# A decoder trunk whose input arrives transposed from the host, with the row norm applied after the first projection

## Chip, core and metric

One core of a Trainium2 chip runs the whole layer in one launch. The metric is device time in microseconds: before, the median of three runs is 781.14 (777.98 to 785.86).

## The reference, cut to what matters

```
u    = x * rsqrt(mean(x*x, -1) + eps) * attn_norm        # x: 1024 rows of 1024
proj = u @ w_in[0]                                       # split into
       # dq dk dv | sq ckv | iq ik iw | rq rk rv | gate
A    = differential attention(dq, dk, dv)                # causal, 6 heads
B    = sparse attention: indexer scores from iq, ik, iw; the 256 best keys of each row
C    = retention(rotary(rq), rotary(rk), rv)             # rotary angles, decays
y    = silu(gate) * concat(A, B, C)
out  = rms_norm(x + y @ w_out[0]) * final_norm
```

Each of the 1024 rows of x has one norm factor. It is common to a whole row, so it can be applied to x before the projection or to a row of the projection after it.

## The kernel before

All products of the projection are made of three matmuls: each operand is split into a high part (rounded to the matmul's format) and a low part (the rest), and high x high, high x low and low x high are added in PSUM. `uh` and `ul` hold the two parts of the normed x, transposed: partitions are 128 of the 1024 model columns (a chunk, k = 0 to 7), free elements are the 1024 rows of x. They stay in SBUF for all units of the projection.

The front. `setup` loads eight row blocks of x (128 rows each, 512 KB) on SyncE's queue; after the second, `wide` puts the weights of the first projection there (columns dv, ik and iw, 456 wide). For each row block `prep_a` squares the rows on ScalarE with a row sum, makes the reciprocal root in `rstd_small` (VectorE and ScalarE in turns on 128x1 operands) and scales the block with norm and gains in one VectorE operation (L213). `prep_b` transposes it with eight TensorE matmuls against the identity into a PSUM tile (L220); ScalarE copies the high part, VectorE subtracts it for the low part (`split`, L113 and L123).

The first projection is unit "a" of `gemm` (L282 to L284): for each row block 24 matmuls with a stationary 128x128 piece of `uh` or `ul` and 456 moving weight columns, accumulated over eight chunks in one PSUM bank. `dv_evac` takes a finished block out: dv and ik by ScalarE (L571, L572), iw by VectorE (L573). After every four blocks the ik part is transposed on TensorE (L578) and split into the keys `kkh` and `kkl`, whose second half of the partitions is filled by two SyncE transfers.

Behind it follow the index units iq0 to iq3 (unit "b" of `gemm`, L130 to L132: 48 matmuls of 512 columns, rows of x as moving operand, in two halves of 512). Their weights come through SyncE and are split on GpSimd (L119, L123). Their results go to DRAM and come back stacked (L305, L318). The index scores (L343, L344) need the keys and iq0. They are interleaved with iq1's successors; then come a top-k search of 31 steps on VectorE and ScalarE, the attention groups with the other units of the projection between them, retention and the output projection.

The order of instructions on each engine is made by a planner that simulates the program with its own costs and picks what is ready by priority. Inside a `manual_schedule` block the named engines keep the order in which the code is written: before, that is TensorE from iq0 to the scores. Tiles of one tag share a number of slots (`bufs`); a new tile waits until the oldest one has been read by all its users. An engine takes its instructions in order, and SyncE and ScalarE each feed a queue of transfers.

Late loads (`setup_late`): small norm vectors, lambda, and a table of rotary angles and decays (`trigdec`, tag `m1`), issued on SyncE.

Of the kernel before, what the change touches and what calls it, by code (L numbers as in the profile page):

```python
# [20 lines left out]
NB = 8  # L21
# [47 lines left out]
class Trunk:  # L69
# [65 lines left out]
    def setup(self):  # L135
        nc, i = self.nc, self.i
        nc.scalar.preload_act_table_set("natural_log_exp_and_others")
        self.ident = self.const("ident", [128, 128])
        make_identity(nc, self.ident)
        self.gb = self.ptile(1024)  # L140
        nc.scalar.dma_start(self.gb, bass.AP(tensor=i["attn_norm"].tensor, offset=i["attn_norm"].offset,
                                             ap=[[0, 128], [1, 1024]]))
        self.x = {}
# [12 lines left out]
        nc.vector.memset(self.ct, 1.0)  # L156
        self.bd = self.const("bd", [128, 128])
        nc.vector.memset(self.bd, 0.0)
        for a in range(2):
            nc.vector.memset(self.bd[a * 64:(a + 1) * 64, a * 64:(a + 1) * 64], 1.0)  # L160

    def setup_late(self):
        nc, i = self.nc, self.i

        def ld(out, in_):
            self.tc.keep_in_program_order(nc.sync.dma_start(out, in_))

# [20 lines left out]
        m1 = self.sb.tile([128, NB, 72], F, name="trigdec", tag="m1")  # L188
        self.trig, self.dec = m1[:, :, 0:64], m1[:, :, 64:72]
        ld(self.trig, i["trig"].rearrange("(b p) c -> p b c", p=128))  # L190
        ld(self.dec, i["decay"].rearrange("(b p) c -> p b c", p=128))

    def rstd_small(self, ss, n, tag):
        nc = self.nc
        w = ss.shape[1]
        t = self.sb.tile([128, 3, w], F, name=self.name("rs"), tag=tag, bufs=2)
        v, r, q = (t[:, j] for j in range(3))
        nc.vector.tensor_scalar(v, ss, 1.0 / n, EPS, op0=OP.mult, op1=OP.add)
        nc.scalar.activation(r, v, AF.Ln)
        nc.scalar.activation(r, r, AF.Exp, scale=-0.5)  # L200
        nc.vector.scalar_tensor_tensor(q, r, v, r, op0=OP.mult, op1=OP.mult)
# [4 lines left out]
    def prep_a(self, b):  # L206
        nc = self.nc
        xt = self.x[b]
        junk = self.half("junk", [128, 1024], BF)
        ss = self.sb.tile([128, 1], F, name=self.name("ss"), tag="ss", bufs=2)  # L210
        nc.scalar.activation(junk, xt, AF.Square, accum_out=ss)
        r = self.rstd_small(ss, D, "rs1")
        nc.vector.scalar_tensor_tensor(xt, xt, r, self.gb, op0=OP.mult, op1=OP.mult)  # L213

    def prep_b(self, b):
        nc = self.nc
        xt = self.x.pop(b)
        p = self.pS()
        for k in range(KC):
            nc.tensor.transpose(p[:, k * 128:(k + 1) * 128], xt[:, k * 128:(k + 1) * 128], self.ident)  # L220
        pv = p.rearrange("p (k s) -> p k s", k=KC)
        sl = slice(b * 128, (b + 1) * 128)
        self.split(self.uh[:, :, sl], self.ul[:, :, sl], pv)

    def wtile(self, base, shape, dt=FR):
        return self.sb.tile([128] + shape, dt, name=self.name(base), tag="w", bufs=NW)
# [2 lines left out]
        return self.sb.tile([128] + shape, F, name=self.name("wr"), tag="wr", bufs=2)  # L229

    def wide(self):
        raws = []
        for k0 in range(0, KC, 2):
            tag, bufs = ("pq", NPQ) if k0 < 2 * NPQ else ("hl", NHL)
            raw = self.sb.tile([128, 2, WA], F, name=self.name("wr"), tag=tag, bufs=bufs)
            for a, b, c in ((0, 384, C_DV), (384, WA, C_IK)):
                self.nc.sync.dma_start(raw[:, :, a:b], self.i["w_in"][
                    0, k0 * 128:(k0 + 2) * 128, c:c + b - a].rearrange("(k p) c -> p k c", p=128))
            raws.append(raw)
        self.dvw = raws  # L240

    def wsplit(self, c0, w):
        hs, ls = [], []
        if w == WA:
# [5 lines left out]
            for k in range(KC):  # L250
                self.split(hs[k], ls[k], self.dvw[k // 2][:, k % 2], *K["s0"][k])
            return hs, ls
        n = 1024 // w
        for k0 in range(0, KC, n):
# [308 lines left out]
    def dv_evac(self):  # L563
        nc = self.nc
        self.v = self.sb.tile([128, NB, 384], F, name=self.name("v"), tag="v")
        self.iw = self.const("iw", [128, NB, 8])
        self.kkh, self.kkl = self.slot("kkh", [128, S], FR), self.slot("kkl", [128, S], FR)
        kt = self.half("kt", [128, NB, 64])

        def evac(b, ps):  # L570
            nc.scalar.activation(self.v[:, b, :], ps[:, 0:384], AF.Copy)  # L571
            nc.scalar.activation(kt[:, b], ps[:, 384:448], AF.Copy)  # L572
            nc.vector.tensor_scalar(self.iw[:, b], ps[:, 448:456], IDX_SCALE, None, op0=OP.mult)  # L573
            if b % 4 == 3:
                sl = slice(b * 128 - 384, b * 128 + 128)
                p = self.pB()
                for j in range(4):
                    nc.tensor.transpose(p[0:64, j * 128:(j + 1) * 128], kt[:, b - 3 + j], self.ident)  # L578
                self.split(self.kkh[0:64, sl], self.kkl[0:64, sl], p[0:64])
            if b == NB - 1:  # L580
                self.mv(self.kkh[64:128], self.kkh[0:64])
                self.mv(self.kkl[64:128], self.kkl[0:64])
        return evac

    def attend(self, pair, stages, GB=2, groups=(3, 2, 1, 0)):
        nc = self.nc
# [244 lines left out]
    def run(self):  # L831
# [148 lines left out]
```

## Time and profile before

| what | value |
|---|---|
| median of three runs | 781.14 us (777.98, 781.14, 785.86) |
| profiled execution | 785.29 us, of which the span of the core is 783.6 |
| TensorE matmul busy | 724.2 us (92%), 4314 instructions |
| VectorE, ScalarE, GpSimd busy | 551.5, 447.6 and 311.5 us |
| moved by DMA | 113.05 MB, mean 144 GB/s |
| granted TensorE clock, mean | 0.974 |

All stretches and dates below are microseconds from the start of the span. In the rows PE is TensorE's matmul, PEld its weight load, DVE is VectorE, ACT is ScalarE, POOL is GpSimd, SPq is SyncE's queue. A matmul's shown duration includes its way through the array, so the pace of a row of matmuls is read from their starts. PEclk is the granted clock as a share of 2.4 GHz.

### The profile page before, as it was taken

The page shows a single profiled execution, that of the slowest core. Times are in us where ns is not written, and L with a number is a line of the kernel's source. Part 1 is how long each engine was busy: PE and PEld are TensorE (multiplying, and loading weights), DVE is VectorE, ACT ScalarE, POOL GpSimd, SP SyncE. Part 2 cuts the span into 40 slices and gives each one's busy share as a digit, 9 for nine tenths or more (in the row PEclk, how much of TensorE's full clock was granted, in tenths as well). Part 3 has the DMA queues.
Part 4 walks back from the last instruction along what each step waited for, and adds up shares of the span by engine and source line. Part 5 has one row for each costly group of instructions (what it writes and reads, how often), then busy time and mean ns, then how long its engine had stood idle before and what let it go on. Part 6 is the DMA issues. An engine that isn't in the chain of part 4 may idle for free.

```text
span 783.6 us, 12891 instructions
## 1 busy us (share of the span) xinstructions
PE 724.2 (92%) x4314; PEld 597.4 (76%) x4314; DVE 551.5 (70%) x1312; ACT 447.6 (57%) x989; POOL 311.5 (40%) x343
## 2 busy tenths in 40 slices
PE   3999999999999999988799789998978999999996
PEld 3798888887887898766577567997855887787884
DVE  5920277789999989999889997325657766664443
ACT  4531255559888968787755566434356656554332
POOL 6401322225434438557347699335733242120000
PEclk9999999999999999999899999999968999999999
DMA  9303645454374352461274476564578974413351
GB/s 332 78 1 71 197 136 145 139 137 132 99 218 115 85 163 78 120 169 35 67 206 144 144 215 190 158 192 160 158 213 236 281 200 127 123 48 108 118 176 59
DMA packets 93250, 113.05 MB, mean 144 GB/s; under 512 B 11904, under 2 KB 63488, under 8 KB 93056
## 3 DMA queue, kind: packets, MB, share of 16 engines
q1 hardware_dynamic: 91888, 109.61, 48.1%
q10 hardware_dynamic: 1296, 2.62, 0.9%
q8 instruction: 34, 0.56, 0.3%
q14 instruction: 32, 0.26, 0.1%
HBM read 75.50 MB, written 36.18 MB: 143 GB/s over the span
## 4 chain that ended last, share of the span: by engine, by line
PE 61%; DVE 16%; DMA 6%; issue 6%; POOL 5%; ACT 4%; SPq 0%; DVEq 0%; POOLq 0%; ACTq 0%
PE pB L626 6%; PE pG L130 6%; PE pG L132 6%; PE pG L131 5%; PE pB L611 4%; PE pG L282 4%; PE pG L936 4%; PE pG L937 4%; PE pG L935 4%; PE pG L283 4%; PE pG L284 4%; DVE jv L378 3%; DMA wr<-in_w_in_dram 2%; PE pS L344 2%; PE pS L343 2%
## 5 line engine op out<-in xcount | busy, mean ns | idle before, releaser
L130 PE MATMUL pG<-uh,wh 128*128 128x512 f32 x352 | 141.6, 402 | 1.8 <-DVE gt L827 1.8
L132 PE MATMUL pG<-uh,wl 128*128 128x512 f32 x352 | 140.7, 400 | 0.6 <-POOL wl L123 0.6
L131 PE MATMUL pG<-ul,wh 128*128 128x512 f32 x352 | 139.4, 396 | 0.0
L123 POOL TENSOR_TENSOR wl<-wr,wh 128x512 fp32r<-128x512 f32 x56 | 79.3, 1430 | 106.3 <-PE pG L131 69.4
L392 ACT ACTIVATE ja<-sc,tk_c 128x896 int8<-128x896 f32 (+2 forms) x93 | 83.2, 895 | 17.3 <-DVE tk_c L399 12.0
L113 ACT ACTIVATE pt<-pB 128x512 f32<-128x512 f32 (+2 forms) x120 | 58.8, 496 | 43.8 <-PE pB L611 43.5
L130 PEld LDWEIGHTS pG<-uh,wh 128*128 128x128 f32 x352 | 66.8, 190 | 16.4 <-DVE gt L827 2.4
L132 PEld LDWEIGHTS pG<-uh,wl 128*128 128x128 f32 x352 | 66.4, 189 | 16.1 <-POOL wl L123 0.9
L611 PE MATMUL pB<-ident,pp 128*128 128x128 f32 x432 | 72.9, 287 | 5.5 <-DVE gt L758 3.4
L626 PE MATMUL pB<-pt,v 128*64 128x128 f32 x864 | 70.8, 302 | 7.6 <-ACT pt L113 7.0
L131 PEld LDWEIGHTS pG<-ul,wh 128*128 128x128 f32 x352 | 66.7, 189 | 13.0 <-issue 0.2
L626 PEld LDWEIGHTS pB<-pt,v 128*64 128x64 f32 x864 | 57.7, 147 | 18.9 <-ACT pt L113 9.5
L378 DVE TENSOR_SCALAR_CACHE_REDUCE jv<-sc,tk_c 128x640 bf16<-128x640 f32 (+4 forms) x81 | 69.2, 855 | 1.0
L611 PEld LDWEIGHTS pB<-ident,pp 128*128 128x128 f32 x432 | 51.2, 144 | 22.2 <-issue 9.1
L677 POOL TENSOR_SCALAR pq<-pq,mx 128x896 f32<-128x896 f32 (+7 forms) x48 | 43.2, 901 | 58.6 <-DVE mx L676 55.8
L119 POOL TENSOR_SCALAR wh<-wr 128x512 fp32r<-128x512 f32 x56 | 37.8, 680 | 59.9 <-DMA wr<-in_w_in_dram 54.3
L282 PE MATMUL pG<-wh,uh 128*128 128x256 f32 x192 | 55.0, 288 | 2.6 <-POOL wh L119 2.6
L283 PE MATMUL pG<-wl,uh 128*128 128x256 f32 x192 | 54.9, 286 | 0.0
L284 PE MATMUL pG<-wh,ul 128*128 128x256 f32 x192 | 54.3, 284 | 0.0
L346 ACT ACTIVATE pp<-pS 128x1024 f32<-128x1024 f32 (+5 forms) x48 | 36.5, 760 | 31.1 <-PE pS L344 31.0
L651 PE MATMUL pS<-st,st 128*128 128x512 f32 (+3 forms) x144 | 43.3, 368 | 11.5 <-DVE mx L662 8.9
L351 DVE SCALAR_TENSOR_TENSOR sc<-pp,iw,sc 128x1024 f32<-128x1024 f32 (+5 forms) x42 | 43.5, 1044 | 14.3 <-ACT pp L346 13.6
(218 smaller groups left out, 1756.1 us busy)
## 6 DMA issues: line engine op xcount, KB each, us to landing
wr<-in_w_in_dram SPq DMA_DIRECT2D x56, 256.0 KB, 3.2
st<-qdq SPq DMA_DIRECT2D x24, 256.0 KB, 4.2
st<-qkk SPq DMA_DIRECT2D x18, 256.0 KB, 5.9
x<-in_x_dram SPq DMA_DIRECT2D x8, 512.0 KB, 6.6
qiq<-hl SPq DMA_DIRECT2D x16, 256.0 KB, 3.5
st<-qiq SPq DMA_DIRECT2D x8, 512.0 KB, 3.3
wr<-in_w_out_dram SPq DMA_DIRECT2D x16, 256.0 KB, 3.4
xr<-in_x_dram SPq DMA_DIRECT2D x8, 512.0 KB, 3.5
```

The source lines that it names most:

```text
L113: self.nc.scalar.activation(out, in_, AF.Copy)
L123: (self.nc.vector if e2 == "v" else self.nc.gpsimd).tensor_tensor(lo, src, hi.bitcast(F), OP.subtract)
L130: mm(ps, wh, xh, start=start, stop=False)
L131: mm(ps, wh, xl, start=False, stop=False)
L132: mm(ps, wl, xh, start=False, stop=stop)
L282: mm(ps, uh, hs[k], start=k == 0, stop=False)
L283: mm(ps, uh, ls[k], start=False, stop=False)
L284: mm(ps, ul, hs[k], start=False, stop=k == KC - 1)
L378: nc.vector.tensor_scalar(jv[:, :nv[b]], hb if b == 7 and bit >= 16 else sc[b], t, 0.0, op0=op, op1=OP.add, accum_out=cnt[:, j:j + 1])
L392: nc.scalar.activation(ja[:, :nv[b]], sc[b], AF.Sign, bias=cut(b), scale=-1.0, accum_out=cnt[:, cols[b]:cols[b] + 1])
L611: nc.tensor.transpose(p[:, k], pr[:, (k0 + k) * 128:(k0 + k + 1) * 128], self.ident)
L626: self.last = nc.tensor.matmul(o[u * 64:(u + 1) * 64], vals[k], pts[g, a][:, k, u * 128:(u + 1) * 128], start=k == (i if u else 0), stop=k ...
```

## The change

- The host passes x transposed as well (`x_t`), `attn_norm` laid out by chunk, and the 456 weight columns of the first projection as one contiguous array (`w_dv`). The latter are loaded on ScalarE's queue, the first two chunks one by one.
- SyncE loads chunk 0 and 1 of `x_t` in halves; then a row block of x behind each further chunk, up to eight. The rows serve the norm alone: ScalarE squares and sums them (`square`).
- `split_x` makes `uh` and `ul` of a chunk from x times gains, without the norm. `front` goes chunk by chunk: six row blocks (18 matmuls a step) accumulate in six PSUM banks at once; then come blocks 6 and 7.
- `diags` makes all norm factors at once, behind the split of the last chunk, and eight diagonal matrices with them; `row_rms` broadcasts the factors over the partitions with eight matmuls.
- `resplit` then scales x by gains and factors and rewrites `uh` and `ul`, half of the columns after blocks 0 to 5, the other half after blocks 6 and 7; iq0 and all later units use these.
- The evictions apply the norm factor and are on ScalarE alone; iw is taken from the ik tile later. The keys' transposes stand behind iq0 (`keys`). Their tile moves to tag `m1`, one slot shared with the table of angles and decays.
- TensorE, VectorE and SyncE keep the written order inside `front`. The weight splits of the first projection use GpSimd and ScalarE, no longer VectorE.

```diff
-K = {... 's0': ('gg', 'gg', 'ag', 'gg', 'vg', 'gg', 'vg', 'vg'), ...
+K = {... 's0': ('gg', 'ag', 'gg', 'ag', 'gg', 'ag', 'gg', 'ag'), ...
...
-        for b in range(NB):
-            self.x[b] = self.slot("x", [128, 1024])
-            nc.sync.dma_start(self.x[b], i["x"][0, b * 128:(b + 1) * 128, :])
-            if b == K["xp"] - 1:
-                self.wide()
+        nc.scalar.dma_start(self.gk, i["attn_norm"])
+        self.wide()
+        self.x, self.rows = [], []
+        self.ss = self.const("ss", [128, NB])
+        for k in range(KC + 1):
+            if k < KC:
+                t = self.slot("x", [128, S])
+                for c in (slice(0, 512), slice(512, S)) if k < 2 else (slice(0, S),):
+                    nc.sync.dma_start(t[:, c], i["x_t"][k * 128:(k + 1) * 128, c])
+                self.x.append(t)
+            for b in ((k - 1,) if 0 < k else ()):
+                row = self.ptile(D) if b % 2 else self.wtile("row", [D], F)
+                nc.sync.dma_start(row, i["x"][0, b * 128:(b + 1) * 128, :])
+                self.rows.append(row)
+                self.square(b)
...
+    def split_x(self, k):
+        g = self.gk[:, k:k + 1]
+        for c in (slice(0, 512), slice(512, S)):
+            hi, x = self.uh[:, k, c], self.x[k][:, c]
+            nc.scalar.activation(hi, x, AF.Copy, scale=g)
+            nc.vector.scalar_tensor_tensor(self.ul[:, k, c], x, g, hi.bitcast(F), op0=OP.mult, op1=OP.subtract)
...
+    def row_rms(self):
+        p = self.pS()
+        for b in range(NB):
+            nc.tensor.matmul(p[:, b * 128:(b + 1) * 128], self.ct, self.dg[b], start=True, stop=True)
+        return p
...
+    def diags(self):
+        self.rn = self.rstd_small(self.ss, D, "rs8")
+        for b in range(NB):
...
+            self.nc.vector.tensor_scalar(self.dg[b], self.ident, self.rn[:, b:b + 1], None, op0=OP.mult)
...
+    def resplit(self, p, half):
+        c = slice(half * 512, half * 512 + 512)
+        for k in range(KC + 1):
+            if k < KC:
+                x = self.x[k][:, c]
+                nc.vector.scalar_tensor_tensor(x, x, self.gk[:, k:k + 1], p[:, c], op0=OP.mult, op1=OP.mult)
+                nc.scalar.activation(self.uh[:, k, c], x, AF.Copy)
+            if k:
+                hi = self.uh[:, k - 1, c]
+                nc.vector.tensor_tensor(self.ul[:, k - 1, c], self.x[k - 1][:, c], hi.bitcast(F), OP.subtract)
...
+    def front(self):
+        big = [self.pS(), self.pS()]
+        ps = [big[b // 2][:, b % 2 * 512:b % 2 * 512 + WA] for b in range(4)] + [self.pB()[:, :WA] for _ in range(2)]
...
+        for k in range(KC):
+            self.split_w(k)
+            self.split_x(k)
+            if k == KC - 1:
+                self.diags()
+            step(range(6), k)
+        for b in range(6):
+            evac(b, ps[b])
+        rb = self.row_rms()
+        self.resplit(rb, 0)
+        ps[6:] = [self.pG()[:, :WA] for _ in range(2)]
+        for k in range(KC):
+            step((6, 7), k)
+        for b in (6, 7):
+            evac(b, ps[b])
+        self.resplit(rb, 1)
...
-            nc.vector.tensor_scalar(self.iw[:, b], ps[:, 448:456], IDX_SCALE, None, op0=OP.mult)
+            nc.scalar.activation(self.v[:, b, :], ps[:, 0:384], AF.Copy, scale=r)
+            nc.scalar.activation(kt[:, b], ps[:, 384:456], AF.Copy, scale=r)
...
-        for b in range(NB):
-            self.prep_a(b)
-            self.prep_b(b)
-        drain(self.gemm(("a", C_DV, WA, self.dv_evac())))
-        with self.tc.manual_schedule(engines={mybir.EngineType.PE}):
-            drain(units("iq0 iq1"))
+        with self.tc.manual_schedule(engines={et.PE, et.DVE, et.SP}):
+            keys = self.front()
+        with self.tc.manual_schedule(engines={et.PE}):
+            drain(units("iq0"))
+            keys()
+            drain(units("iq1"))
```

## Rows read from the trace of the kernel before

**Rows 1.** Page, part 4: shares of the chain that ended last, by engine.
```profile
PE 61%; DVE 16%; DMA 6%; issue 6%; POOL 5%; ACT 4%; SPq 0%; DVEq 0%; POOLq 0%; ACTq 0%
```

**Rows 2.** Windows of the front: stretch, length, busy per engine (count), PEclk, DMA share, GB/s.
```profile
0.00:5.00 5.00, 0.00 (x0) 0.00 (x0) 0.63 (x10) 1.28 (x1) 1.83 (x8) 1.00 0.53 179
5.00:20.00 15.00, 7.84 (x30) 6.98 (x31) 10.58 (x16) 7.64 (x15) 10.61 (x11) 1.00 1.05 384
31.50:36.00 4.50, 4.47 (x19) 3.89 (x20) 4.50 (x17) 2.84 (x7) 0.00 (x0) 0.62 0.02 5
36.00:67.10 31.10, 31.10 (x166) 28.07 (x166) 8.31 (x16) 6.71 (x14) 1.25 (x2) 1.00 0.00 1
```

**Rows 3.** Windows of the score stage and of a later, attention stage.
```profile
100.00:120.00 20.00, 20.00 (x95) 16.72 (x94) 14.28 (x15) 11.18 (x16) 4.81 (x4) 1.00 0.50 151
320.00:360.00 40.00, 33.55 (x185) 25.25 (x182) 37.90 (x98) 33.58 (x79) 18.41 (x21) 0.96 0.44 119
```

**Rows 4.** Timeline of TensorE: start, length, engine, line, operation, tiles.
```profile
15.72 0.73 PE L282 MATMUL pG<-wb,uh 128*128 128x456 f32 x1
...
19.13 0.58 PE L282 MATMUL pG<-wb,uh 128*128 128x456 f32 x2
...
50.22 0.37 PE L283 MATMUL pG<-wb,uh 128*128 128x456 f32 x1
...
56.42 0.37 PE L283 MATMUL pG<-wb,uh 128*128 128x456 f32 x1
...
67.10 0.39 PE L130 MATMUL pG<-uh,wh 128*128 128x512 f32 x1
...
78.36 0.40 PE L130 MATMUL pG<-uh,wh 128*128 128x512 f32 x1
```

**Rows 5.** Timeline of one block's norm and transposes; waits (total, times, longest).
```profile
7.19 0.15 DVE L198 TENSOR_SCALAR rs<-ss 128x1 f32<-128x1 f32 x1 [5.53 <-ACT junk L211]
...
8.49 1.28 DVE L213 SCALAR_TENSOR_TENSOR x<-x,rs,pp 128x1024 f32<-128x1024 f32 x1
...
24.03 1.07 PE L220 MATMUL pS<-ident,x 128*128 128x128 f32 x8
...
PE pS L220 <- DVE rs L198: 11.0, 2, 9.9
```

**Rows 6.** Timeline: first data, late loads, iq1's weights; median landing of weight loads.
```profile
6.01 1.06 ACT L211 ACTIVATE junk<-x 128x1024 bf16<-128x1024 f32 x1 [3.93 <-DMA x<-in_x_dram]
...
9.39 1.35 POOL L119 TENSOR_SCALAR wb<-wr 128x456 fp32r<-128x456 f32 x2 [6.92 <-DMA wr<-in_w_in_dram]
...
23.27 0.43 SPq L166 DMA_DIRECT2D trigdec<-in_trig_dram  x1
...
25.04 2.33 SPq L258 DMA_DIRECT2D wr<-in_w_in_dram  x2
...
wr<-in_w_in_dram SPq DMA_DIRECT2D x56, 256.0 KB, 3.2
```

**Rows 7.** Groups by line and form: busy us, mean ns of one, idle before.
```profile
L941 ACT ACTIVATE z<-xr 128x512 bf16<-128x512 f32 x16 | 10.1, 630 | 31.1 <-DVE xr L939 30.6 <-ACT xr L951 0.5
L211 ACT ACTIVATE junk<-x 128x1024 bf16<-128x1024 f32 x8 | 8.3, 1044 | 3.9 <-DMA x<-in_x_dram 3.9
L953 DVE SCALAR_TENSOR_TENSOR xr<-xr,rs,fn 128x512 f32<-128x512 f32 x8 | 6.0, 751 | 0.3
L943 DVE TENSOR_TENSOR xr<-xr,fn 128x512 f32<-128x512 f32 x8 | 5.5, 689 | 3.7 <-ACT z L941 3.7
L123 DVE TENSOR_TENSOR hl<-pG,hl 128x512 fp32r<-128x512 f32 x20 | 13.7, 685 | 14.9 <-ACT hl L113 14.9
L123 POOL TENSOR_TENSOR wl<-wr,wh x6: 1278/1290/2123, 22.9 to 79.7; 128x512 fp32r<-128x512 f32 x6
```

**Rows 8.** By tile: shortest, median and longest ns, first and last start, form.
```profile
L213 DVE SCALAR_TENSOR_TENSOR x<-x,rs,pp x8: 1283/1446/2410, 8.5 to 37.9; 128x1024 f32<-128x1024 f32 x8
L123 DVE TENSOR_TENSOR ul<-pS,uh x8: 1204/1219/1225, 14.7 to 49.1; 128x1024 fp32r<-128x1024 f32 x8
```

More of the change, by code (lines that the diff above doesn't have):

```diff
@@ L139, in setup @@
         make_identity(nc, self.ident)
[L140 to L143, printed above, removed]
-        for b in range(NB):
-            self.x[b] = self.slot("x", [128, 1024])
-            nc.sync.dma_start(self.x[b], i["x"][0, b * 128:(b + 1) * 128, :])
-            if b == K["xp"] - 1:
-                self.wide()
+        self.gk = self.const("gk", [128, KC])
+        nc.scalar.dma_start(self.gk, i["attn_norm"])
[13 more added lines that the diff above has]
+                self.square(b)
         self.uh = self.sb.tile([128, KC, S], FR, name="uh", tag="uh")
@@ L187, in setup_late @@
         nc.vector.tensor_scalar(self.nlam, self.nlam, -LAM_INIT, None, op0=OP.add)
-        m1 = self.sb.tile([128, NB, 72], F, name="trigdec", tag="m1")
+        m1 = self.sb.tile([128, NB, 72], F, name="trigdec", tag="m1", bufs=1)
         self.trig, self.dec = m1[:, :, 0:64], m1[:, :, 64:72]
@@ L200, in rstd_small @@
         nc.scalar.activation(r, r, AF.Exp, scale=-0.5)
-        nc.vector.scalar_tensor_tensor(q, r, v, r, op0=OP.mult, op1=OP.mult)
+        if w == 1:
+            nc.vector.scalar_tensor_tensor(q, r, v, r, op0=OP.mult, op1=OP.mult)
+        else:
+            nc.vector.tensor_tensor(q, r, r, OP.mult)
+            nc.vector.tensor_tensor(q, q, v, OP.mult)
         nc.vector.tensor_scalar(q, q, -0.5, 1.5, op0=OP.mult, op1=OP.add)
@@ L216, in prep_b, with square @@
+    def square(self, b):
+        junk = self.half("junk", [128, D], BF)
+        self.nc.scalar.activation(junk, self.rows[b], AF.Square, accum_out=self.ss[:, b:b + 1])
+    def row_rms(self):
         nc = self.nc
-        xt = self.x.pop(b)
         p = self.pS()
-        for k in range(KC):
[L220 to L223, printed above, removed]
+        for b in range(NB):
+            nc.tensor.matmul(p[:, b * 128:(b + 1) * 128], self.ct, self.dg[b], start=True, stop=True)
+        return p
@@ new lines, in front, with step @@
+    def front(self):
+        nc = self.nc
+        hs, ls = self.wsplit(C_DV, WA)
+        evac, keys = self.dv_evac()
+        mm = nc.tensor.matmul
+        big = [self.pS(), self.pS()]
+        ps = [big[b // 2][:, b % 2 * 512:b % 2 * 512 + WA] for b in range(4)] + [self.pB()[:, :WA] for _ in range(2)]
+        ps += [None, None]
+        def step(blocks, k):
+            st, sp = k == 0, k == KC - 1
+            todo = [[(b, self.uh, hs, st, False) for b in blocks], [(b, self.uh, ls, False, False) for b in blocks],
+                    [(b, self.ul, hs, False, sp) for b in blocks]]
+            order = [t for b in zip(*todo) for t in b] if sp else [t for w in todo for t in w]
+            for b, u, w, s0, s1 in order:
+                mm(ps[b], u[:, k, b * 128:(b + 1) * 128], w[k], start=s0, stop=s1)
+        for k in range(KC):
+            self.split_w(k)
[13 more added lines that the diff above has]
+        self.resplit(rb, 1)
+        return keys
@@ L235, in wide @@
             raw = self.sb.tile([128, 2, WA], F, name=self.name("wr"), tag=tag, bufs=bufs)
[L236 to L240, printed above, removed]
+            for j in ((0, 1), (1, 2)) if k0 < 2 else ((0, 2),):
+                self.nc.scalar.dma_start(raw[:, j[0]:j[1]], self.i["w_dv"][
+                    (k0 + j[0]) * 128:(k0 + j[1]) * 128].rearrange("(k p) c -> p k c", p=128))
+            self.dvw.append(raw)
     def wsplit(self, c0, w):
@@ L249, in wsplit @@
             ls = [big[2 + k // 2][:, k % 2] for k in range(KC)]
-            for k in range(KC):
-                self.split(hs[k], ls[k], self.dvw[k // 2][:, k % 2], *K["s0"][k])
+            self.split_w = lambda k: self.split(hs[k], ls[k], self.dvw[k // 2][:, k % 2], *K["s0"][k])
             return hs, ls
@@ L566, in dv_evac, with keys @@
         self.iw = self.const("iw", [128, NB, 8])
-        self.kkh, self.kkl = self.slot("kkh", [128, S], FR), self.slot("kkl", [128, S], FR)
-        kt = self.half("kt", [128, NB, 64])
+        kt = self.sb.tile([128, NB, 72], F, name="kt", tag="m1", bufs=1)
         def evac(b, ps):
-            nc.scalar.activation(self.v[:, b, :], ps[:, 0:384], AF.Copy)
-            nc.scalar.activation(kt[:, b], ps[:, 384:448], AF.Copy)
-            nc.vector.tensor_scalar(self.iw[:, b], ps[:, 448:456], IDX_SCALE, None, op0=OP.mult)
-            if b % 4 == 3:
-                sl = slice(b * 128 - 384, b * 128 + 128)
+            r = self.rn[:, b:b + 1]
+            nc.scalar.activation(self.v[:, b, :], ps[:, 0:384], AF.Copy, scale=r)
+            nc.scalar.activation(kt[:, b], ps[:, 384:456], AF.Copy, scale=r)
+        def keys():
+            self.kkh, self.kkl = self.slot("kkh", [128, S], FR), self.slot("kkl", [128, S], FR)
+            nc.vector.tensor_scalar(self.iw, kt[:, :, 64:72], IDX_SCALE, None, op0=OP.mult)
+            for h in range(2):
+                sl = slice(h * 512, h * 512 + 512)
                 p = self.pB()
                 for j in range(4):
-                    nc.tensor.transpose(p[0:64, j * 128:(j + 1) * 128], kt[:, b - 3 + j], self.ident)
+                    nc.tensor.transpose(p[0:64, j * 128:(j + 1) * 128], kt[:, 4 * h + j, 0:64], self.ident)
                 self.split(self.kkh[0:64, sl], self.kkl[0:64, sl], p[0:64])
[L580 to L583, printed above, removed]
+            self.mv(self.kkh[64:128], self.kkh[0:64])
+            self.mv(self.kkl[64:128], self.kkl[0:64])
+        return evac, keys
     def attend(self, pair, stages, GB=2, groups=(3, 2, 1, 0)):
@@ L969 @@
     host["trig"], host["decay"] = _tables()
+    host["x_t"] = np.ascontiguousarray(np.asarray(inputs["x"])[0].T)
+    host["attn_norm"] = np.ascontiguousarray(np.asarray(inputs["attn_norm"])[0].reshape(KC, 128).T)
+    w = np.asarray(inputs["w_in"])[0]
+    host["w_dv"] = np.ascontiguousarray(np.concatenate([w[:, C_DV:C_DV + 384], w[:, C_IK:C_IK + 72]], 1))
     arrays, ins = {}, {}
```

18 lines of the change are left out of this document (8 added, 10 removed).

## The prediction

> **What bounds the kernel now.** I read the page first: TensorE holds 61% of the chain that ended last [rows 1], so the end moves with what TensorE does or waits for. Then the windows by stage. From 36 to 67 us it is busy without a gap [rows 2]; in the score stage after it too, and in the top-k and attention stages it and VectorE are both near full [rows 3]. Nothing there is tied to a date of its own: scores need iq0 and the keys, the top-k needs the scores. The change touches the stretch before, so I look for the date at which TensorE reaches the second index unit, iq1.
>
> The timeline gives it. The first matmul of the first projection starts at 15.72, the first of iq0 at 67.10, the first of iq1 at 78.36 [rows 4]. The projection is 192 matmuls. At full pace 30 of them take 6.20 us (50.22 to 56.42), 0.207 each, so 192 need 39.7 of these 51.4 us. The rest is transposes of x, 48 in this stretch at 1.07 us for eight [rows 5], 6.4; two stretches at about half pace, the first with nine matmuls in 3.41 us (15.72 to 19.13) [rows 4], 1.6 lost, the second where the granted clock of 31.5 to 36 is 0.62, so mostly the level of 1.2 GHz [rows 2], after TensorE had had little to do; and the gap of some 2 us before that. Ahead of 15.72 TensorE has done 16 transposes and else nothing, because norm, scaling, transposition and split of a row are a chain through four engines: its wait for the norm is 9.9 us at the longest [rows 5].
>
> **The change, part by part.** Dates are on the clock of the profiled execution.
>
> *Start.* Transposed x needs neither norm nor transposition: 64 transposes leave TensorE. The first operand is the scaled copy of half a chunk (256 KB). Before, the first row of 512 KB was there at 6.01, with 512 KB of gains moved beside it [rows 6]; half of that beside 234 KB of weights should be there near 5; the copy takes 0.63 (128x512 on ScalarE) [rows 7]. GpSimd's first weight copy is 0.67 (two in 1.35 [rows 6]). I take the first matmul at 6.3. Ends: 5.3, and 10.1 if weights come no earlier than now (9.39, plus 0.7). ScalarE now issues six transfers first, SyncE 18; at 0.43 for one [rows 6] that is 2.6 and 7.7 us, ScalarE's ahead of the first data, SyncE's ahead of all but the first chunks.
>
> *Eight steps of 18 matmuls.* 144 x 0.207 = 29.8, plus one stretch at half pace, 1.6: the last step ends at 37.7; one lasts 3.72. Beside it must fit, of each chunk: ScalarE two copies and a square (1.04 and a short read-out), every second time a weight copy (0.63 at most), 2.8 on average; VectorE two operations of 0.75, 1.5; GpSimd at most 0.67 + 1.29 [rows 7]. They fit. Transfers: 0.9 MB are in by 5 us, then 384 GB/s [rows 2]; x twice and the weights are 10.26 MB, so the last row lands at 5 + 9.36/0.384 = 29.4, and chunk 2, all weights interleaved, at 13.0, needed at 15.3. These are the covers; without them each microsecond of delay is one of TensorE's.
>
> *Norms.* Behind the last row a square of 1.2; the short operations took 1.3 from sum to scale (7.19 to 8.49 [rows 5]) and get one more, 0.2; eight 128x128 scalings, some 0.35 each by the slope from 512 columns to 1024 (0.75 to 1.28 [rows 7, 8]), 2.8. Ready at 34.9, cover 2.8 us. An eviction is at most two copies of 0.63, on ScalarE; blocks 0 and 1 are evicted inside the last step, and that frees the PSUM tile for the eight broadcast matmuls. I cost these as transposes, 0.13 each, 1.0: 38.7. VectorE's eight small evictions go; they were on no path.
>
> *Blocks 6 and 7.* 48 x 0.207 = 9.9: until 48.6. Meanwhile VectorE rescales the first half of the columns: eight scalings with one operand in PSUM, not shown before, 0.75 as from SBUF (ends 0.68, the subtraction from PSUM, and 1.2, half of the 1024-wide worst case), and eight subtractions at 0.69 [rows 7, 8]: 11.5, from 38.5 to 50.0. ScalarE's copies (0.63) hide in the skew of one chunk.
>
> *iq0.* Its first half, 24 matmuls, runs from 48.9 to 54.5. The second half needs the second rescaling, again 11.5, to 61.5: VectorE, not TensorE, ends iq0, at 62.0. GpSimd works beside it on iq1's low part and iq2's high part, 2 x 1.29 + 2 x 0.67 = 3.9 us. The row scaling of before took 1.28 at best and 2.41 at worst, while the subtraction with an operand in PSUM stayed within 1.20 to 1.23 [rows 8]; so only eight of the 16 operations of a half should suffer, and I add 1.5.
> The Trainium skill ("SBUF — State Buffer", section "SBUF: two separate sides") says that a VectorE operation with two SBUF inputs and a GpSimd operation that reads SBUF exclude each other for a whole instruction; the spread of rows 8 agrees, and by it up to 3.9 would be added in place of 1.5, the forecast becoming 769.6.
> iq0 ends at 63.5, the keys' eight transposes, now behind it, take 1.0, and iq1 starts at 64.5 instead of 78.36: **13.9 us earlier**. The transfers of keys and of iq0's parts lie beside iq1's 11.3 us as now (iq0's length, 67.10 to 78.36).
>
> *Late loads.* The table of angles now shares a slot with the keys and waits, on SyncE, for their transposes. Behind it would be weights and stores of the index units. I cost it at nothing as long as it is queued where the slot comes free; if not, see the third rival.
>
> **Sum.** The profiled execution took 785.3 (span 783.6), 0.5% above the median of 781.1: 785.3 - 13.9 = 771.4, and on the median's scale 781.1 - 13.9 = **767**.
>
> **Rivals.**
> *VectorE becomes the bound of the front* (the other side). Place: the rescalings, 38.5 to 61.5. If all 32 operations ran at the worst ratio of [rows 8], 2.41/1.28 = 1.88, the 23.0 us become 43.3; iq1 starts at 83.3, and iq0 in trickles at the lower clock adds 1.6: 6.5 later than now, 788. The sign turns at a mean ratio of about 1.6. For: VectorE has no slack there. Against: GpSimd has 3.9 us of work in these 23, and reads of PSUM were not stretched. 8%.
> *The norms are late, so the change does not do what it says.* Below 9.36/(32.2 - 5) = 344 GB/s they end behind the last step. At 300 the last row is in at 36.2, the norms at 41.7: 4.0 late, 1.6 more at the lower clock, gain 8.3: 773. For: the first 5 us average only 179 [rows 2]. Against: 15 us at 384, with small pieces among them. 12%.
> *SyncE's order.* Before, the late loads (23.27) stand ahead of iq1's weights (25.04) [rows 6]. If they stay there, iq1's weights wait for the keys' transposes at 64.5, then 3.2 to landing and 3.9 on GpSimd: iq1 at 71.6, 1.6 for the clock, gain 5.2: 776. A new order may cost as much further on, where TensorE is idle 6 of 40 us [rows 3]. For: everything behind the front is ordered anew. Against: the planner reckons with the slot. 14%.
>
> **Numbers.** The sum as worked: 66%, own range 761 to 772 (start 1 earlier or 3.7 later, no collisions or 3.9, 3 either way for a new order). The range for 8 in 10 takes in the second and third rivals: 759 to 777. Within 1% (7.8 us) a measurement of this kernel tells no change; faster means under 773.3: the 66% and half of the second rival, 72%. Within: the other half, most of the third, 18%. Slower: the first and the third's tail, 10%.
>
> **What would show it.** Right: first projection matmul near 6; no gap between steps up to 38; broadcast matmuls not waiting for norms; VectorE without idle time from 38 to 62; iq1 at 64 to 65; the same offset at the first score and at the end. Wrong: a second stretch at the lower clock, splits waiting for chunks, subtractions far above 0.7 with iq0 behind them, iq1's weights late, or an offset at iq1 that is gone at 500 us.

## The result: 1.5% faster, 12 us of the 13.9 forecast

The changed kernel takes 771.84 us (median of four runs, 769.08 to 772.95); the kernel before 783.5 (four runs, 777.98 to 787.67: the three of the section on the time before, and one more). The ratio is 0.9845, 95% interval 0.9811 to 0.9878. The forecast was 767, range 759 to 777, with 72% on faster by over 1%: range and direction held, the point was 5 us low. The profiled executions are 785.29 and 772.95, spans 783.6 and 771.2: 12.4 us. The mean granted clock is the same in both, 0.974 before and 0.973 after, so the gain is not a luckier clock over the run.

I read after in the order in which I read before: the shares of the chain of waits, then the windows of the front (columns as in [rows 2]), then TensorE's timeline.

```profile
PE 62%; DVE 13%; DMA 8%; issue 7%; ACT 4%; POOL 4%; SPq 2%; ACTq 0%; DVEq 0%; POOLq 0%
```
```profile
0.00:5.00 5.00, 0.00 (x0) 0.00 (x0) 0.63 (x10) 1.28 (x1) 1.83 (x8) 1.00 0.58 177
5.00:20.00 15.00, 13.45 (x53) 12.12 (x54) 6.60 (x6) 8.84 (x16) 11.02 (x11) 1.00 1.02 394
31.50:36.00 4.50, 4.50 (x23) 4.09 (x22) 1.83 (x5) 1.57 (x4) 3.28 (x4) 1.00 0.37 89
12.84:38.94 26.10, 26.10 (x128) 23.62 (x127) 15.78 (x28) 18.63 (x37) 14.71 (x14) 1.00 0.80 289
51.12:64.65 13.53, 12.21 (x49) 8.63 (x50) 12.30 (x20) 6.65 (x12) 1.62 (x2) 1.00 0.27 71
100.00:120.00 20.00, 20.00 (x96) 16.87 (x95) 15.60 (x17) 10.98 (x15) 5.99 (x5) 1.00 0.49 133
```

Against [rows 1, 2, 3]: TensorE still holds the chain, and the score stage looks as it did. The difference lies in the front: between 5 and 20 us TensorE was busy 7.84, now 13.45, and the stretch of 31.5 to 36 has the full granted clock where it had 0.62. In iq0 (51.12 to 64.65) TensorE has gaps (busy 12.21 of 13.53), and VectorE is busy 12.30 of the 12.91 us up to its last subtraction, which ends at 64.03.

TensorE's timeline (start, length, operation, count, idle before):

```profile
6.55 1.86 PE L272 MATMUL pS<-wb,uh 128*128 128x456 f32 x4 [6.55 <-ACT uh L222]
...
12.84 0.37 PE L272 MATMUL pS<-wb,uh 128*128 128x456 f32 x1
...
38.94 1.95 PE L233 MATMUL pS<-dg,ct 128*128 128x128 f32 x16
40.64 1.07 PE L272 MATMUL pG<-wb,uh 128*128 128x456 f32 x4
...
51.12 0.47 PE L130 MATMUL pG<-uh,wh 128*128 128x512 f32 x1 [0.31 <-POOL wl L123]
...
64.65 1.03 PE L646 MATMUL pB<-ident,kt 128*64 128x128 f32 x8
65.44 0.47 PE L130 MATMUL pG<-uh,wh 128*128 128x512 f32 x1
...
76.48 0.47 PE L408 MATMUL pS<-kkh,st 128*128 128x512 f32 x1
...
148.97 0.33 PE L408 MATMUL pS<-kkh,st 128*128 128x384 f32 x1
...
589.32 0.50 PE L1003 MATMUL pG<-woh,yh 128*128 128x512 f32 x1 [1.68 <-ACT yh L113]
```

In the kernel before, the three marks that [rows 4] does not have, the first and last score and the first matmul of the output projection, are

```profile
89.52 0.39 PE L343 MATMUL pS<-kkh,st 128*128 128x512 f32 x1
...
161.63 0.33 PE L343 MATMUL pS<-kkh,st 128*128 128x384 f32 x1
...
602.55 0.50 PE L935 MATMUL pG<-woh,yh 128*128 128x512 f32 x1 [1.44 <-ACT yh L113]
```

So the offset is 12.9 us at iq1 (78.36 against 65.44), 13.0 at the first score, 12.7 at the last, 13.2 at the output projection and 12.4 at the end. The gain is made in the first 65 us and carried to the end. Where it is made follows from the same marks: the first projection matmul comes 9.17 earlier (15.72 against 6.55), the stretch from there to iq0 is 6.81 shorter (51.38 against 44.57), iq0 is 2.27 longer (11.26 against 13.53), and the keys' transposes, now behind it, take 0.79; together 12.9. No run takes the two halves of the change, x transposed by the host and the norm applied later, apart.

### The profile page after: what moved, and what is told of

The parts are those of the page before. It is cut to its first block, busy times and chain, and to the rows that moved or that the text cites. A ratio compares the mean times of both kernels' runs of the same rounds, so it can differ in the third digit from the quotient of the medians.

```text
span 771.2 us, 12824 instructions
## 1 busy us (share of the span) xinstructions
PE 718.2 (93%) x4266; PEld 591.1 (77%) x4266; DVE 559.9 (73%) x1315; ACT 458.6 (59%) x1002; POOL 310.4 (40%) x343
## 4 chain that ended last, share of the span: by engine, by line
PE 62%; DVE 13%; DMA 8%; issue 7%; ACT 4%; POOL 4%; SPq 2%; ACTq 0%; DVEq 0%; POOLq 0%
PE pG L130 6%; PE pG L131 6%; PE pG L132 6%; PE pB L693 5%; PE pB L678 4%; PE pG L1003 4%; PE pG L1004 4%; PE pG L1005 4%; PE pS L272 3%; PE pG L347 2%; DVE jv L443 2%; PE pG L349 2%; PE pG L348 2%; PE pS L409 2%; PE pS L408 2%
## 5 line engine op out<-in xcount | busy, mean ns | idle before, releaser
L693 PE MATMUL pB<-pt,v 128*64 128x128 f32 x864 | 68.0, 294 | 7.4 <-ACT pt L113 6.8
L693 PEld LDWEIGHTS pB<-pt,v 128*64 128x64 f32 x864 | 55.3, 143 | 18.9 <-ACT pt L113 9.5
L119 POOL TENSOR_SCALAR wh<-wr 128x512 fp32r<-128x512 f32 x56 | 40.3, 723 | 69.9 <-DMA wr<-in_w_in_dram 50.8
L744 POOL TENSOR_SCALAR pq<-pq,mx 128x896 f32<-128x896 f32 (+7 forms) x48 | 39.2, 816 | 58.5 <-DVE mx L743 46.1
L411 ACT ACTIVATE pp<-pS 128x1024 f32<-128x1024 f32 (+5 forms) x48 | 36.5, 760 | 31.5 <-PE pS L409 31.5
L747 DVE SCALAR_TENSOR_TENSOR pp<-pp,mx,pq 128x896 f32<-128x896 f32 (+7 forms) x48 | 51.1, 1065 | 4.4 <-POOL pq L744 3.6
```

Of the source, the lines that this page charges most:

```text
L693: self.last = nc.tensor.matmul(o[u * 64:(u + 1) * 64], vals[k], pts[g, a][:, k, u * 128:(u + 1) * 128], start=k == (i if u else 0), stop=k ...
```

## Experiments

Times of single runs are that of the profiled execution; dates are read from TensorE's timeline as above. "iq1" is the start of the second index unit, "broadcast" that of the eight matmuls of `row_rms`. One kernel's executions differ by some us (after: 769.08 to 772.95), so single times say less than dates. In the expectations "theory" is the account under test, "rival" the one against it.

**e1: the weight load alone.** The kernel before, with the contiguous weights of the change on ScalarE's queue and its split of the weight copies:

```
-    for a, b, c in ((0, 384, C_DV), (384, WA, C_IK)):
-        self.nc.sync.dma_start(raw[:, :, a:b], w_in[...])
+    for j in ((0, 1), (1, 2)) if k0 < 2 else ((0, 2),):
+        self.nc.scalar.dma_start(raw[:, j[0]:j[1]], w_dv[...])
```

> The kernel before with one part of the change alone: the first projection's weights come as one contiguous array on ScalarE's queue and are split without VectorE; the norm still precedes the transposes. Theory (the gain is TensorE no longer waiting for norm, scaling and transposes): the first projection still starts near 15 us and iq1 comes at 74 to 78 (before: 78.4, changed: 65.4), the time is 0 to 0.5% under the kernel before. Rival (the gain is the cheaper weight transfers and the relief of VectorE): iq1 at 70 or earlier, and more than 1% under the kernel before.

Measured: 791.31 us (four runs, 783.93 to 794.51) against 784.46, ratio 1.0108 (1.0051 to 1.0166): slower, which neither expected. The profiled execution is the fastest of the four, and in it iq1 comes 3.8 later than before, at 82.17, where theory had said 74 to 78:

```profile
82.17 0.40 PE L130 MATMUL pG<-uh,wh 128*128 128x512 f32 x1
```

ScalarE's own timeline says why (an ACTq row is the issue of transfers):

```profile
1.26 7.55 ACTq L236 DMA_DIRECT2D wr<-in_w_dv_dram  x5
8.86 1.06 ACT L210 ACTIVATE junk<-x 128x1024 bf16<-128x1024 f32 x1 [6.77 <-DMA wr<-in_w_dv_dram]
```

Five issues take 7.55 us: three are out by 3.1, the last starts only at 8.4, and ScalarE computes nothing in that time. The first square starts at 8.86 instead of 6.01 [rows 6], with a weight transfer as releaser, the first transposes at 15.42, the projection at 20.40. The rival, that the weights are the gain, is not borne out. TensorE's longest wait is for a norm again, 15.4 us where [rows 5] had 9.9, so the norm chain is still the bound. But e1 pays for ScalarE's held start, so it does not give the price of an early weight load without that cost. The changed kernel issues in the same way (4.37 us of issues for these weights ahead of its first ScalarE operation); what that costs there is told under "Start" below.

**e2: late norms.** Six more squares behind the last row (`for _ in range(6): self.square(NB - 1)`), whose results are thrown away.

> The changed kernel with the square of the last row block done six more times, 7.4 us of ScalarE's, so that the norms come later by that. Theory (the norms' only cover is the end of the last step: factors spread into diagonals at 38.3, wanted at 38.9): the broadcast matmuls start 6 to 7 us later, near 45.5, iq1 near 72 to 74, the time 7 to 9 us over the changed kernel. Rival (VectorE's rescaling or the transfers bound the front, the norms have cover to spare): iq1 moves by less than 3 us.

```profile
42.15 1.66 DVE L245 TENSOR_SCALAR dg<-ident,rs 128x128 f32<-128x128 f32 x8
```
```profile
43.67 3.57 PE L235 MATMUL pS<-dg,ct 128*128 128x128 f32 x16 [5.13 <-DVE dg L245]
46.99 1.07 PE L274 MATMUL pG<-wb,uh 128*128 128x456 f32 x4
```
```profile
43.60:47.00 3.40, 3.33 (x17) 3.33 (x17) 0.88 (x6) 2.84 (x10) 0.00 (x0) 0.52 0.01 2
```

TensorE waits 5.13 us for the diagonals, and the 16 passes behind that wait take 3.3 us instead of 1.7, at a granted clock of 0.52, the level of 1.2 GHz. The broadcast starts 4.7 later than in after (43.67 against 38.94) and ends 6.4 later (46.99 against 40.64), iq1 comes at 70.96 (+5.5), and the time is 776.83 (one run; +5.0 on after's median). Theory had 6 to 7, 72 to 74 and 7 to 9, so all three fell short, though the sum of squares was 7.0 later (40.59 against 33.55), near the 7.4 that I had reckoned. The difference lies behind the sum: the short operations and the diagonals took less than in after, where GpSimd works beside them (see "Norms" below):

```profile
40.59 0.17 DVE L207 TENSOR_SCALAR rs<-ss 128x8 f32<-128x8 f32 x1 [9.46 <-ACT junk L229]
```

So the wait for the norms is real, and it is paid twice, as idle time and as clock.

**e3: no subtractions in the second half's rescaling** (`if k:` becomes `if k and not half:`; the low part of the second half is left out).

> The changed kernel without the subtraction for the low part in the second rescaling: rows 512 to 1023 of the normed x keep the low part of the unscaled x, all eight subtractions (5.5 us of VectorE) are left out. Theory (VectorE ends iq0: TensorE waits there for it): iq0's second half runs without gaps, iq1 starts 2.0 to 2.6 us earlier, near 63, and the first score too, near 74. Rival (those waits are hidden, the first score hangs on something else): the first score stays at 76.5 within 0.5 us.

iq1 starts at 62.98, 2.46 earlier, with TensorE waiting for no subtraction: VectorE ends iq0. But the first score comes at 75.24, only 1.24 earlier, because a new wait ends last there:

```profile
75.24 0.47 PE L408 MATMUL pS<-kkh,st 128*128 128x512 f32 x1 [1.08 <-DMA st<-qiq]
```

That is the load of iq0's result, which goes out to memory and back. The time is 768.52. Both accounts were half right: theory for iq1, neither for the score.

**e5: three of these subtractions on GpSimd** (`eng = nc.gpsimd if half and k in (2, 4, 6) else nc.vector`).

> The changed kernel with three of the eight subtractions of the second rescaling on GpSimd instead of VectorE. Theory (VectorE's queue ends iq0): 2.0 us less on VectorE, iq0 and iq1 1 to 2 us earlier, iq1 at 63.5 to 64.5. Rival (the two engines exclude each other on these operations, so the work does not run beside): iq1 at 65.4 or later.

iq1 at 64.19, 1.25 earlier, as theory had it; the first score at 76.23, 0.25 earlier, behind 0.9 us of the same wait; 770.58 us.

**e6: the small evictions back on VectorE**, the weights of the index heads straight from PSUM:

```
-    nc.scalar.activation(kt[:, b], ps[:, 384:456], AF.Copy, scale=r)
+    nc.scalar.activation(kt[:, b, 0:64], ps[:, 384:448], AF.Copy, scale=r)
+    nc.vector.tensor_scalar(self.iw[:, b], ps[:, 448:456], r, IDX_SCALE, op0=OP.mult, op1=OP.mult)
```

> The changed kernel with iw evicted by VectorE again, block by block, and ScalarE's second copy 64 instead of 72 wide: the evictions part undone. Theory (eight operations of about 0.17, before each rescaling, where VectorE waits for the broadcast anyway): iq1 within 0.7 us of 65.4. Rival (the evictions on ScalarE alone carry part of the gain): iq1 later by 2 us or more.

```profile
40.13 2.02 PE L233 MATMUL pS<-dg,ct 128*128 128x128 f32 x16 [1.34 <-DVE iw L638]
...
53.81 0.47 PE L130 MATMUL pG<-uh,wh 128*128 128x512 f32 x1 [1.72 <-DVE iw L638]
```

Eight operations of 0.2 us on VectorE, for which TensorE waits at the broadcast and at iq0 to get a PSUM tile back, make the broadcast 1.2 us later and iq0 2.7. Most of that is hidden again behind VectorE's rescaling, so iq1 moves by 0.76, just past theory's 0.7; the first score moves by 2.0, the time to 777.12 (one run). The rival's 2 us at iq1 did not come, but my step that the evictions "were on no path" is true only of the kernel before.

**e4: constant matmuls ahead of the first projection.**

```
+    warm = self.pG()
+    for _ in range(22):
+        mm(warm[:, :128], self.ct, self.ct, start=True, stop=True)
```

> The changed kernel with 22 matmuls on constants (128 columns) put on TensorE ahead of the first step, to lift its clock before the first data are there. The first step lasted 6.3 us instead of 3.7 at the lower pace. Rival (each step is TensorE's alone): 2.4 us earlier from step 1 on, iq1 at 63.0. Theory (the steps' cover was thin: ScalarE takes the late weight chunks in order, ahead of chunks 2 and 3, whose copies were ready at 15.4 and 20.0 where TensorE wanted them at 16.6 and 20.3): step 2 waits over 1 us and step 3 starts no earlier than 20.0, iq1 at 65.0 to 65.4.

```profile
1.12 7.67 PE L264 MATMUL pG<-ct 128*128 128x128 f32 x44 [1.12 <-DVE ct L163]
```

Each of these f32 matmuls is two passes (x44 for 22), which I had not reckoned with, so the projection started 2 us late, at 8.55. Its first step then took 3.80 us (to 12.35) instead of 6.29: the lower pace is a cost of the first microseconds of activity, and constants can bear it. Broadcast at 38.49, iq1 at 65.13, 768.85 us (one run). That iq1 lies in theory's 65.0 to 65.4 is luck: no step waited, and step 3 started at 19.84, where theory had said not before 20.0; the late start had taken the time.

**e7, e8: the same with all weight copies on GpSimd, and e8 also with the last row in a tile that nobody holds.**

> As e4_warm, and all weight splits on GpSimd, so that ScalarE no longer waits for late weights ahead of chunks 2 and 3. Theory: the steps run without gaps from 6.5 on and end near 36.4, 2.5 us earlier; then the broadcast matmuls wait for the norms, whose last row block was asked for at 29.1 only: they start at 38.4 to 39, iq1 at 64.6 to 65.2, so most of the gain is a new wait. Rival (the norms have cover): iq1 at 63.0.

> As e7_warm_gg, and the last row block gets a place of its own, so that its load is queued ahead of the index weights and the small late loads. Theory: norms 5 us or more earlier, the broadcast matmuls follow the last step near 36.4 without a wait, iq1 near 63.0, the first score near 74, the end 2 to 2.5 us under the changed kernel. Rival (the norms are not what e7_warm_gg waits for): as e7_warm_gg.

e7: broadcast 38.61, iq1 65.14, 777.41 us. e8: 38.25, 64.80, 774.26. The late start of e4 is in both, so they did not test the covers: e7's dates fit theory, but the steps ended near 38.6, not 36.4, and e8 missed theory's 63.0 by that start. They showed something else: e7 has e4's iq1 to 0.01 us and ends 8.6 us later.

**e9, e10, e11: twelve constants, in time; with both edits of e8; with e5's edit.**

> The changed kernel with twelve constant matmuls (24 passes) ahead of the first projection. Theory (the lower clock cost step 0 of the first projection 2.57 us, and the covers of steps 2 and 3 are only about 1 us): the passes end near 6.3, step 0 starts at 6.6 and runs at full pace to 10.4, TensorE then waits 1.0 to 1.5 us at step 2 (its first copy is ready near 15.4) and 0.5 to 1.0 at step 3 (20.0), so that the broadcast starts at 38.2 to 38.8 instead of 38.94 and iq1 at 64.8 to 65.4 instead of 65.44. Rival (the clock alone sets the date): no wait at steps 2 and 3, the broadcast at 36.4 if the norms allow it, at 38.2 if not, with one wait of 1.8 us right ahead of it. Time: theory within 0.5% of the changed kernel.

> As e9, with all the weight splits on GpSimd and row 7 loaded into a tile that waits for nobody. Theory (three thin covers behind one another: clock, weight copies, norms): with all three lifted the broadcast starts at 36.4 to 37.4 and iq1 at 63.0 to 64.2; the time 768 to 773, since the order behind the front moves by some us from kernel to kernel. Rival (the copies of the chunks, one an engine each 0.65 us, or the loads of the chunks hold the steps): waits of over 0.5 us at steps 1 to 7 remain, the broadcast not before 38.

> As e9, with three of the second half's eight subtractions on GpSimd. Theory (iq1 hangs on the second half's rescaling, whose start hangs on the broadcast): iq1 1.25 us earlier than in e9, as those three subtractions alone gave, thus 63.6 to 64.2; the first score 0.2 to 1.0 earlier. Rival (TensorE's own 48 matmuls of iq0 end last): iq1 unchanged against e9 within 0.3.

e9's timeline, rows with a wait ahead of steps 2 and 3; then the broadcast of e10 and the iq1 of e10 and e11:

```profile
1.13 4.77 PE L264 MATMUL pG<-ct 128*128 128x128 f32 x24 [1.13 <-DVE ct L163]
6.46 1.07 PE L275 MATMUL pS<-wb,uh 128*128 128x456 f32 x4 [0.56 <-ACT uh L222]
...
14.88 1.09 PE L275 MATMUL pS<-wb,uh 128*128 128x456 f32 x4 [0.30 <-ACT uh L222]
...
19.54 1.10 PE L275 MATMUL pS<-wb,uh 128*128 128x456 f32 x4 [0.68 <-ACT uh L222]
```
```profile
37.26 2.05 PE L237 MATMUL pS<-dg,ct 128*128 128x128 f32 x16 [0.65 <-ACT kt L643]
...
63.84 0.48 PE L130 MATMUL pG<-uh,wh 128*128 128x512 f32 x1
```
```profile
63.18 0.48 PE L130 MATMUL pG<-uh,wh 128*128 128x512 f32 x1
```

| | broadcast | iq1 | first score | last score | output projection | span | mean clock | median us | ratio to before (95%) |
|---|---|---|---|---|---|---|---|---|---|
| before | - | 78.36 | 89.52 | 161.63 | 602.55 | 783.6 | 0.974 | | |
| after | 38.94 | 65.44 | 76.48 | 148.97 | 589.32 | 771.2 | 0.973 | 771.84 | 0.9845 (0.9811 to 0.9878) |
| e4 | 38.49 | 65.13 | 77.50 | 148.91 | 585.32 | 767.1 | 0.980 | one run | |
| e7 | 38.61 | 65.14 | 78.18 | 151.25 | 592.34 | 775.7 | 0.973 | one run | |
| e9 | 38.29 | 64.80 | 77.46 | 148.89 | 591.38 | 773.3 | 0.971 | 777.09 | 0.9888 (0.9854 to 0.9922) |
| e10 | 37.26 | 63.84 | 76.16 | 147.58 | 585.58 | 767.4 | 0.978 | 771.12 | 0.983 (0.9786 to 0.9875) |
| e11 | 38.28 | 63.18 | 75.64 | 147.05 | 586.61 | 768.4 | 0.977 | 771.24 | 0.9821 (0.9785 to 0.9856) |

The 2.5 us that step 0 loses to the lower pace are worth 0.65 at the broadcast (e9), because the steps behind then run into their covers. The waits shown are 0.3 and 0.7, where theory had said 1.0 to 1.5 and 0.5 to 1.0; steps 1 and 2 together take 9.27 us (10.27 to 19.54) instead of 7.46, which is the 1.8 that is missing. With the weight copies and the last row out of the way too, these waits are gone and the broadcast is 1.7 earlier than in after, as theory had it (e10). Its one wait left is for an eviction, and the eviction waits for the norm factors:

```profile
34.49 1.15 DVE L218 TENSOR_TENSOR rs<-rs 128x8 f32<-128x8 f32 x1
```
```profile
35.73 0.58 ACT L642 ACTIVATE v<-pS,rs 128x384 f32<-128x384 f32 x1 [2.96 <-DVE rs L218]
```

e11's iq1 is 1.6 earlier than e9's, theory's way but further than its 63.6 to 64.2; the first score is 1.8 earlier, where theory had 0.2 to 1.0. The front thus moves as the covers say, not always by the size. But none of these versions is measurably faster than the changed kernel: up to 2.3 us at iq1 are within the intervals.

## Why the prediction was right, and where its sizes were off

**Start.** Forecast 6.3, measured 6.55, but not as worked. The first half chunk, issued at 0.81, landed 3.0 us later, at 3.8 and not near 5. ScalarE could not copy it then, because its six issues of transfers lasted until 5.64, 4.8 us where I had reckoned 2.6:

```profile
1.27 4.37 ACTq L304 DMA_DIRECT2D wr<-in_w_dv_dram  x5
5.68 1.33 ACT L222 ACTIVATE uh<-x,gk 128x512 fp32r<-128x512 f32 x2 [3.60 <-DMA wr<-in_w_dv_dram]
```

So the early data and the longer issues cancelled, and the date is in part luck.

**Lower pace.** Forecast 1.6 lost, measured 2.57: the first 18 matmuls took 6.29 (6.55 to 12.84), against 3.72 for a step. I took the loss from nine matmuls in [rows 4], where 16 transposes had gone before. It is not one figure: with the same front, step 0 took 5.16 in e2, 5.95 in e6, 6.22 in e3 and 6.42 in e5, so between 1.4 and 2.7 us are lost from one execution to the next, and 2.57 is the figure of this one. e4 confirms the cause by taking it away.

**Steps 1 to 7.** No gap: 126 matmuls from 12.84 to 38.94, 0.207 each. But the covers were far thinner than my average of 2.8 us of ScalarE a chunk. ScalarE runs its queue in order, and a weight copy that waits for its transfer stands ahead of the chunk's copies:

```profile
14.26 0.59 ACT L113 ACTIVATE wb<-wr 128x456 fp32r<-128x456 f32 x1 [1.75 <-DMA wr<-in_w_dv_dram]
14.75 1.32 ACT L222 ACTIVATE uh<-x,gk 128x512 fp32r<-128x512 f32 x2
```

The first copy for step 2 is ready near 15.4 and wanted at 16.56; that for step 3 near 20.0, wanted at 20.3. That the steps fitted was partly the 2.57 us lost at step 0: in e2, where step 0 ended 1.3 earlier, step 2 took 4.33 us instead of 3.74.

**Norms.** Forecast ready 34.9 with a cover of 2.8; the cover was 0.6. SyncE's timeline and the three engines behind it:

```profile
22.49 3.64 SPq L173 DMA_DIRECT2D c_diff_norm<-in_diff_norm_dram  x2
...
29.13 0.35 SPq L153 DMA_DIRECT2D pp<-in_x_dram  x1
```
```profile
32.37 1.06 ACT L227 ACTIVATE junk<-pp 128x1024 bf16<-128x1024 f32 x1 [1.55 <-DMA pp<-in_x_dram]
```
```profile
36.31 2.02 DVE L243 TENSOR_SCALAR dg<-ident,rs 128x128 f32<-128x128 f32 x8
```

I had bounded this by the rate of the transfers (344 GB/s decides), and the rate was there, 394 between 5 and 20 us. What was late was the issue: of SyncE's 18 issues, which I had put at 7.7 us, the last row's goes out at 29.13, the time at which I had it landed. It stands behind small late loads on the same queue; its tile is the fourth of a tag with three places, so it needs the square of row block 1 to be done. The second part is behind the sum, where I had 1.5 us for the short operations; they took 2.8 (33.55 to 36.31), and two of them were stretched beside GpSimd's split of the index units' weights (0.92, and 0.61 at 35.59):

```profile
33.55 0.92 DVE L205 TENSOR_SCALAR rs<-ss 128x8 f32<-128x8 f32 x1 [2.45 <-ACT junk L227]
```
```profile
33.15 1.29 POOL L123 TENSOR_TENSOR wl<-wr,wh 128x512 fp32r<-128x512 f32 x1
```

In e2, where GpSimd had nothing to do at that time, the same operation took 0.17; in e10 its neighbours took up to 1.15 and the factors came 3.6 us after the sum (32.05 to 35.64). So the collisions that I had put into the rescalings alone also lie on the norms' path; no run moved the weight split away to test it. The second rival came within 0.6 us of being true, for reasons that I had not named. e2 shows what it would have cost, e10 that the norms are also what holds the next improvement. SyncE is held further by transfers of the other queue:

```profile
SPq L149 <- DMA wr<-in_w_dv_dram: 7.2, 4, 2.8
```

(total, times, longest): its issues of x wait, 7.2 us in all, for ScalarE's weights to land. This is the step "SyncE's order" of the third rival, at another place than I put it; iq1's weights, which I feared for, were in time.

**Broadcast.** Forecast 1.0, measured 1.70: 8 matmuls are 16 passes of 0.106. I had costed them as transposes of x, 0.13 each, where each of these f32 matmuls is two passes. Start 0.25, pace 0.97 and broadcast 0.70 make 1.9, which is the way from 38.7 forecast to 40.64 measured.

**Blocks 6 and 7, iq0.** 48 matmuls took 9.93, as forecast. iq0 starts at 51.12, 0.55 behind the last of them, because its PSUM tile waits for ScalarE's eviction of block 6, which ends at 51.02; forecast 48.9. The row names GpSimd's low part as releaser, which ends at 51.04; in e2 that was done at 57.40, the eviction at 58.26, and iq0 started at 58.36, so it is the eviction.

**VectorE.** Forecast 38.5 to 63.0 (with 1.5 us of collisions); it ran from 40.92, when the broadcast was there, to 64.03. So it started 2.4 late and was 1.4 us shorter, 23.1 instead of 24.5:

```profile
L251 DVE SCALAR_TENSOR_TENSOR x<-x,gk,pS 128x512 f32<-128x512 f32 x16 | 11.7, 741 | 2.2 <-PE pS L233 2.2
L255 DVE TENSOR_TENSOR ul<-x,uh 128x512 fp32r<-128x512 f32 x16 | 12.0, 748 | 0.5 <-ACT uh L252 0.3
```

Durations of neighbours overlap by 0.08: one pair starts 1.26 after the other (44.30, 45.56, 46.82, 48.08), not 1.44. The operation with an operand in PSUM costs 0.741, so the value of 0.75 from SBUF was the right end. In the first rescaling there were two collisions, both beside GpSimd's low part:

```profile
48.05 2.99 POOL L123 TENSOR_TENSOR wl<-wr,wh 128x512 fp32r<-128x512 f32 x2 [9.80 <-PE pG L272]
```
```profile
47.48 0.69 DVE L255 TENSOR_TENSOR ul<-x,uh 128x512 fp32r<-128x512 f32 x1
...
48.74 1.16 DVE L255 TENSOR_TENSOR ul<-x,uh 128x512 fp32r<-128x512 f32 x1
```

0.69 becomes 1.16 and 1.11, together 0.9 us, while the scalings between them stay at 0.74 and 0.75. The rule of the Trainium skill ("SBUF — State Buffer", section "SBUF: two separate sides"), that a VectorE operation with two SBUF inputs and a GpSimd operation that reads SBUF exclude each other, agrees in kind. The worst case of 3.9 did not come, nor my 1.5.

TensorE's wait for these subtractions is what ends iq0 (`DVE ul` 1.3 us, beside waits of the weight loads):

```profile
PE pG L131 <- DVE ul L255: 1.3, 4, 0.4
```

iq0 ends at 64.65, forecast 63.5; the keys take 0.79, forecast 1.0; iq1 at 65.44, forecast 64.5. e3 and e5 confirm the bound. That iq1 came within 1 us is in part luck: the late start of the rescaling (2.4) and its shorter run (1.4) pull in opposite directions.

**The end.** Of the 4.8 us between 767 and 771.84, 1.0 is this; 0.5 more is lost behind iq1 (12.4 instead of 12.9). 2.4 is the base: I put the gain on a median of three runs, 781.1, and a fourth run (787.67) made it 783.5. The last 0.9 or so is the place of the profiled executions among their runs and rounding. The ends that I named for the own range do not add up to it: 1 earlier, no collisions and 3 for the order give 761, but 3.7 later, 3.9 of collisions and 3 for the order give 776, not 772. The result lies within either.

**The rivals.** VectorE did become the bound of iq0, but at a mean ratio near 1.0, not 1.6. The norms were in time, barely. The planner's new order cost nothing that shows in this pair. e4 and e7 have the same iq1 and end 8.6 us apart, 2.3 of it at the last score and 7.0 at the output projection. Much of that goes with TensorE's granted clock. e7 waits 1.87 us for the load of iq0's result (e4: 1.22), and then stands at the level of 1.2 GHz, where e4 reads 1.00:

```profile
78.30:81.70 3.40, 3.40 (x9) 2.66 (x10) 0.50 (x1) 1.02 (x1) 1.24 (x2) 0.50 0.80 224
```

Over the whole span the mean clock leaves out 15.3 us in e4 (767.1 x 0.020) and 20.9 in e7 (775.7 x 0.027), so some 5.6 of the 8.6. Taken off each span in this way, after, e4, e9, e10 and e11 come to 750 to 752, e7 to 755 and before to 763. This is an estimate, because it takes all time at the lower level to lie on the chain; how far the order makes these stretches, and how far chance, stays open. My 3 us either way for a new order took in neither.

## What to carry to other kernels

Where one engine runs the chain without gaps, find the date at which it reaches the first work that the change does not touch: an offset there is the gain, and marks further on (first score, output projection, end) tell whether it lasts. A cover worked out from mean loads and transfer rates is too wide: follow every queue in its written order to the one operation that is last (here a row issued at 29.13 behind small loads, copies behind a weight that had not landed, and short norm operations beside another engine's work). When a front has several thin covers behind one another, lifting one gives little (2.5 us of pace were worth 0.65); and gains of 1 to 2 us are below what the remainder moves by itself, with its order and its granted clock.

## What the runs showed of the hardware that I had not expected

- TensorE starts at half pace, the level of 1.2 GHz, though the granted clock of that stretch reads 1.00: in after the matmuls of 456 columns came 0.38 apart (four in 10.48 - 8.96 = 1.52) until 12.00, then 0.207. The trace's records of the granted clock begin only there, at 12.02 and at full speed; before the first record the column shows 1.00. In e4 the constants ran from 1.12 at 0.213 a pass until 6.40, then at 0.112, and the records begin at 6.39. In e2, with after's front, the pace rose at 9.3. At the start of a program the pace of the matmuls tells, not that column.
- An f32 matmul of 128 columns shows as two passes (x44 for 22 matmuls, x16 for 8) of together 0.21 us; those of 456 and 512 columns in the split form show as one each, 0.207 for 456 columns.
- VectorE operations on 128x8 elements took 0.17 us in e2 and up to 0.92 (after) and 1.15 (e10) while GpSimd subtracted beside them.
- Transfers issued by ScalarE can hold ScalarE's computing (7.55 us of issues in e1) and SyncE's issues as well (7.2 us in after). I read this from the releasers in the trace; what makes an issue wait for an earlier transfer is open.
